# A hybrid mixer layer: another order of the output product's parts, raw weights of the last product in the space of earlier ones, and factor work kept behind the weights

## The chip, the cores and the metric

One core of a Trainium2 chip. The metric is the device time of one execution in microseconds; of several executions the median is given. The engines are TensorE (PE, matmuls), VectorE (DVE), ScalarE (ACT), GpSimd (POOL) and SyncE (SP), each with a queue of instructions that it works off in order. SP issues nearly all loads, POOL the stores that are spoken of below.

## The reference

One decoder layer on 1024 tokens of width 1024, all in float32:

```python
mod = c_act @ w_ada[l] + b_ada[l]
h = rms_norm(x) * (1.0 + scale1) + shift1
proj = h @ w_in[l]
y_ssd = ssd_branch(...)
y_mlstm = mlstm_branch(...)
merged = g_ssd * (y_ssd @ w_branch_ssd[l]) + g_mlstm * (y_mlstm @ w_branch_mlstm[l])
x = x + gate1 * (merged @ w_out[l])
h2 = rms_norm(x) * (1.0 + scale2) + shift2
gt, up = jnp.split(h2 @ w_ffn_in[l], 2, axis=-1)
x = x + gate2 * ((jax.nn.silu(gt) * up) @ w_ffn_out[l])
return rms_norm(x) * final_norm_w
```

The two branches are a Mamba-2 scan and an xLSTM matrix memory. The five large products behind them (`w_branch_ssd`, `w_branch_mlstm`, `w_out`, `w_ffn_in`, `w_ffn_out`) are what the change is about.

## The kernel before

**Number format.** Each float32 operand of a product is split into a high part (a cast on ACT to a rounded 32-bit form, `fp32r`) and the rest (a subtraction on DVE), and each product is three matmuls: high by high, high by rest, rest by high. For the input projection `split` does this for a raw tile of weights (`raw` into `wh` and `wl`, lines 124 and 125).

**Strassen's scheme.** The large products are done in seven part products of half the size each way instead of eight. The sums of weight blocks (S1 to S4) and plain blocks (A11, A12, A22) are the factors. They are prepared ahead, while the mixers run from about 623 to 1385 us: `prep_steps` loads two rows of blocks (`pr`, lines 197 and 198), makes four sums on DVE (lines 210 to 213), and `put_pair` casts, subtracts and stores each factor (lines 162 to 164) through one of two `pf` buffers into DRAM (`fac_ssd`, `fac_ml`, `fac_out`, `fac_ffn`; `f1_d` for part of `w_ffn_in`). Of `w_ffn_out` the blocks A11, A12, A22 aren't stored as factors, and `strassen` loads them raw (`wt`, line 850) and splits them on the way.

**The products.** `strassen` (line 831) goes through the parts in the given `order`. For each of them it takes weights `wf` and tokens `tf` (cast on ACT at line 825, subtraction on DVE at line 826), runs 12 matmuls for each block row `k` (line 879) into four PSUM banks, and hands each bank to a `sink` that adds it to sums. The output product runs from 1909 to 1988 us, and `out_sink` makes the new residual `x1` from it: tokens 0 to 511 are complete after part 4, tokens 512 to 1023 after part 5. Behind it `feat` transposes a block of 128 features of 512 tokens on PE (line 272) and ACT copies it out with scale and shift (line 273) into one of five `f` buffers. The eight features of the first half are split into `h0` and also stored to `f0_d` (line 1124), and those of the second half enter a loop of four rounds (lines 1132 to 1148) that loads the first half again (`b11`, `b21`, lines 1134 and 1135) and builds the token factors `tf` for FFN-in. `head` computes, for the first rows of FFN-in, the two parts that need only the first half.

**FFN-in** (2065 to 2440 us) loads raw columns (`rw`) of each next block, makes their sums on POOL (lines 1109 to 1112), splits them into `sw`, and runs five parts for each block (line 1074); the gated result goes to `act_d` in DRAM (lines 1182 and 1189). The FFN-out product loads it again (`bt`, line 1213) and ends in the final norm.

**What sets the order.** The program is written as one sequence, and a scheduler with a timeline model puts the instructions of each engine in order, within the dependencies; the pools decide in which space a tile lies, and a tile whose space was another's waits until that is free. `tc.issue_after(x)` keeps what is written inside it behind `x` in that order.

Of the kernel before, what the change touches and what calls it, by code (L numbers as in the profile page):

```python
# [9 lines left out]
F32 = mybir.dt.float32  # L10
# [5 lines left out]
P = 128  # L16
# [21 lines left out]
def hybrid_layer(ctx: ExitStack, tc: tile.TileContext, a: dict, out: bass.AP, dbg=None):  # L38
# [27 lines left out]
    def f(ap):  # L66
        return ap.bitcast(F32)
# [50 lines left out]
    V.tensor_scalar(cact, cact, 0.5, None, MUL)  # L118


    def split(raw):
        wh = wp.tile([P, 1024], F32R, name="wh", bufs=NWH)
        wl = wp.tile([P, 1024], F32R, name="wl", bufs=NWL)
        A.copy(wh, raw)  # L124
        V.tensor_tensor(wl, raw, f(wh), SUB)  # L125
        return wh, wl
# [4 lines left out]
    def wload(src):  # L131
        raw = raw_tile()
        Q.dma_start(k8(raw), src.rearrange("(k p) n -> p k n", p=P))
        wh, wl = split(raw)
        return k8(wh), k8(wl)
# [24 lines left out]
    def put_pair(dst, r):  # L160
        m = pf()
        A.copy(m[:, 0], r)  # L162
        V.tensor_tensor(m[:, 1], r, f(m[:, 0]), SUB)  # L163
        G.dma_start(dst, f(m))
# [23 lines left out]
    def prep_steps(name, gate=None):  # L188
        fd, w_d = fac_d[name], w_of[name]
        n = fd.shape[0]  # L190

        def put(r, kk, fa):
            put_pair(fd[kk, FA[fa]], r)

        for kk in range(n):
            r0, r1 = ld("pr"), ld("pr")
            Q.dma_start(r0, w_d[kk * P:(kk + 1) * P, :])
            Q.dma_start(r1, w_d[(kk + n) * P:(kk + n + 1) * P, :])
            if gate is not None:
                g = f(pf()).rearrange("p two n -> p (two n)")  # L200
                Q.dma_start(g, gr_d[gate:gate + 1, :].broadcast_to([P, D]))
                for r in (r0, r1):
                    V.tensor_tensor(r, r, g, MUL)
                yield
            a11, a21, a12, a22 = r0[:, 0:512], r0[:, 512:], r1[:, 0:512], r1[:, 512:]
            if fd.shape[1] == 7:
                for fa, x in (("A11", a11), ("A12", a12), ("A22", a22)):
                    put(x, kk, fa)
                    yield
            V.tensor_tensor(a22, a21, a22, ADD)  # L210
            V.tensor_tensor(a21, a11, a21, SUB)
            V.tensor_tensor(a11, a22, a11, SUB)  # L212
            V.tensor_tensor(a12, a12, a11, SUB)
            yield
            for fa, x in (("S2", a11), ("S3", a21), ("S4", a12), ("S1", a22)):
                put(x, kk, fa)
                yield
# [612 lines left out]

    def strassen(name, load, order, sink, wq, nw, tq, nt, wt_, t2_, rows=False, odd=0):

# [166 lines left out]
    x1 = {}  # L999
    U, U3, R = {}, {}, {}  # L1000

# [21 lines left out]
    def out_sink(p, i, bank):  # L1023
        if p == 1:
            U[i] = ut()
            A.copy(U[i], bank)
            V.tensor_tensor(x1_half(0, i, 0), U[i], x_rows(0, i, 0), ADD)
        elif p == 3:
            R[i] = po.tile([P, 512], F32, name="r", tag="r", bufs=4)
            V.tensor_tensor(R[i], bank, x_rows(1, i, 0), ADD)  # L1030
        elif p == 2:
            x1_part(0, i, 0, bank, x1_half(0, i, 0))
        elif p == 6:
            V.tensor_tensor(U[i], bank, U[i], ADD)
        elif p == 7:
            U3[i] = ut()
            V.tensor_tensor(U3[i], bank, U[i], ADD)
            V.tensor_tensor(x1_half(0, i, 1), U3[i], x_rows(0, i, 1), ADD)
            V.tensor_tensor(R[i], R[i], U[i], ADD)
            V.tensor_tensor(U3[i], U3[i], x_rows(1, i, 1), ADD)  # L1040
        elif p == 4:
            x1_part(0, i, 1, bank, x1_half(0, i, 1))
            x1_done(0, i)
        else:
            x1_part(1, i, 0, bank, R[i])
            x1_part(1, i, 1, bank, U3[i])
            x1_done(1, i)

    strassen("out", lambda k, i, j: am[k + 4 * i], (1, 3, 2, 6, 7, 4, 5), out_sink, wq, 6, tq, 5, None,
             lambda: po.tile([P, 512], F32, name="t2", tag="t2", bufs=2), rows=True)  # L1050
    ctxO.close()
    ctxU.close()


# [63 lines left out]

    f0_d = tc.dram_tile([KD, P, 512], F32, name="f0_d")
    h0 = []  # L1120
    for k in range(KD):
        t = feat(0, k)
        h0.append(split_pair(t, hlo, "h0", "h0", KD))
        G.dma_start(f0_d[k], t)
    w5 = []
    for fa in ("S2", "S3", "S1", "A22", "S4"):
        m = ps_.tile([P, 2, 512], F32R, name="sw", tag="sw", bufs=5)
        Q.dma_start(f(m), f1_d[0, FA[fa]])
        w5.append((m[:, 0], m[:, 1]))
    heads = [head(j) for j in range(NHEAD)]  # L1130
    tf = {n: [] for n in ("t2", "t3", "t1", "t4", "b22")}
    for k in range(4):
# [64 lines left out]
    wq, tq = pool(ctx, "wring"), pool(ctx, "tring")  # L1197
    pb = [pool(ctx, "b0"), pool(ctx, "b1")]
    po = pool(ctx, "fin", "right")
    g2 = po.tile([P, D], F32, name="g2")  # L1200
    Q.dma_start(g2, gr_d[1:2, :].broadcast_to([P, D]))
    fw = po.tile([P, D], F32, name="fw")
    Q.dma_start(fw, a["final_norm_w"].unsqueeze(0).broadcast_to([P, D]))
    ssf = [po.tile([P, 4, 8], F32, name=f"ssf{i}") for i in range(2)]
    yts = [po.tile([P, 1024], F32, name="yt", tag="yt", bufs=8) for _ in range(8)]
    V2, V3 = {}, {}
    acts = {}

# [13 lines left out]
    def y_part(tj, i, ci, bank, u, x=None):  # L1222

        y = yts[4 * tj + i][:, halves(ci)]
        if x is None:
            V.tensor_tensor(y, bank, g2[:, halves(ci)], MUL)
            x = u
        else:
            V.tensor_tensor(y, bank, u, ADD)
            V.tensor_tensor(y, y, g2[:, halves(ci)], MUL)  # L1230
        V.tensor_tensor(y, y, x, ADD)
        half_square(po, yts[4 * tj + i], ssf[tj][:, i], ci)

    def y_done(tj, i):
        yt, ss, t = yts[4 * tj + i], ssf[tj][:, i], 4 * tj + i
        row_rms(ss)
        for ci in range(2):
            ns = halves(ci)
            V.scalar_tensor_tensor(yt[:, ns], yt[:, ns], ss[:, 3:4], fw[:, ns], MUL, MUL)
            Q.dma_start(out[0, t * P:(t + 1) * P, ns], yt[:, ns])  # L1240

    def ffn_sink(p, i, bank):
# [10 lines left out]
        elif p == 5:  # L1253
            V.tensor_tensor(V2[i], bank, V2[i], ADD)
            y_part(1, i, 1, bank, V3[i], x1_rows(1, i, 1))
            V.tensor_tensor(V2[i], V2[i], g2[:, L_], MUL)
            V.tensor_tensor(V2[i], V2[i], x1_rows(1, i, 0), ADD)
# [3 lines left out]
        else:  # L1261
            y_part(1, i, 0, bank, V2[i])
            y_done(1, i)

    strassen("ffn", act_load, ORDER, ffn_sink, wq, 5, tq, 6, lambda: po.tile([P, 512], F32, name="wt", tag="wt", bufs=4),
             lambda: po.tile([P, 512], F32, name="t2", tag="t2", bufs=1), rows=True)
# [23 lines left out]
```

## Time and profile before

| | |
|---|---|
| time, median of 3 runs | 2674.37 us (2671.96 to 2679.69) |
| the profiled execution, its time | 2680.4 us |
| its span | 2678.7 us |
| mean granted clock of TensorE | 0.978 |
| PE busy | 2535.8 us (95%) |
| DVE busy | 1771.2 us (66%) |
| ACT busy | 1102.3 us (41%) |
| POOL busy | 439.9 us (16%) |
| DRAM traffic over the span | 180 GB/s |

A busy share is a mean over the whole span. PE isn't busy for 2678.7 - 2535.8 = 142.9 us of it, spread over stretches with different limits; the rows below are taken from three of them.

### The profile page before, as it was taken

What the parts mean: (1) busy time and instruction counts of PE and PEld (TensorE: products, weight loads), DVE (VectorE), ACT (ScalarE), POOL (GpSimd) and SP (SyncE); (2) the same over time, 40 slices, a digit from 0 to 9 for tenths busy, and PEclk for the clock granted to TensorE, in tenths of its full rate; (3) what the DMA queues carried; (4) which work ended last, traced back from release to release, by engine and by line L of the source; (5) the groups of instructions that cost most, each with busy time, mean ns of one, the idle gap of its engine ahead of it and who ended that gap; (6) DMA issues with size and microseconds to landing.
All of it is one profiled execution on the core that took longest, in us unless ns stands there. A gap on an engine that the chain in (4) does not pass through costs nothing.

```text
span 2678.7 us, 35176 instructions
## 1 busy us (share of the span) xinstructions
PE 2535.8 (95%) x12907; PEld 2117.0 (79%) x12907; DVE 1771.2 (66%) x2885; ACT 1102.3 (41%) x2016; POOL 439.9 (16%) x508
## 2 busy tenths in 40 slices
PE   5999999999999998999999989999998999997998
PEld 3788777888878797888789877878876888886886
DVE  8577767786787567657653537575767666666847
ACT  5455544453444344444443444443244322322323
POOL 4000112110142111212211310000011333231000
PEclk9999999999999999999999999999999999998999
DMA  6323332355778877766753366754773433326655
GB/s 201 102 83 115 114 106 84 110 170 183 233 257 286 287 233 252 257 231 206 248 196 93 116 243 223 268 190 158 249 263 120 126 97 116 101 88 241 218 167 195
DMA packets 342965, 484.04 MB, mean 181 GB/s; under 512 B 21985, under 2 KB 224065, under 8 KB 342793
## 3 DMA queue, kind: packets, MB, share of 16 engines
q1 hardware_dynamic: 309752, 364.87, 43.3%
q0 software_dynamic: 33040, 116.93, 11.6%
q8 instruction: 101, 1.65, 0.3%
q14 instruction: 72, 0.58, 0.1%
HBM read 343.01 MB, written 138.72 MB: 180 GB/s over the span
## 4 chain that ended last, share of the span: by engine, by line
PE 56%; issue 16%; DMA 11%; DVE 9%; ACT 4%; POOL 3%; SPq 0%; POOLq 0%; DVEq 0%; ACTq 0%
PE mm L364 14%; PE n L879 10%; PE n L1074 8%; PE mm L879 5%; PE sc L879 5%; PE mm L1074 4%; PE sc L1074 4%; PE mm L642 2%; DMA ab<-acs_d 1%; DMA raw<-in_w_in_dram 1%; DMA pr<-in_w_ffn_out_dram 1%; ACT ab L546 1%; DVE red L231 1%; DMA fac_out<-pf 1%; PE n L573 1%
## 5 line engine op out<-in xcount | busy, mean ns | idle before, releaser
L364 PE MATMUL mm<-hh,wh 128*128 128x512 f32 x1392 | 557.8, 401 | 15.1 <-ACT xf L378 9.6
L364 PE MATMUL mm<-hh,wl 128*128 128x512 f32 x1392 | 554.3, 398 | 0.0
L364 PE MATMUL mm<-hl,wh 128*128 128x512 f32 x1392 | 553.4, 398 | 0.0
L364 PEld LDWEIGHTS mm<-hh,wh 128*128 128x128 f32 x1392 | 266.1, 191 | 72.8 <-ACT xf L378 11.8
L364 PEld LDWEIGHTS mm<-hh,wl 128*128 128x128 f32 x1392 | 265.8, 191 | 53.2 <-DVE wl L125 0.7
L364 PEld LDWEIGHTS mm<-hl,wh 128*128 128x128 f32 x1392 | 265.9, 191 | 51.8 <-issue 0.2
L125 DVE TENSOR_TENSOR wl<-raw,wh 128x1024 fp32r<-128x1024 f32 x122 | 151.6, 1243 | 89.5 <-PE mm L642 26.1
L124 ACT CAST wh<-raw 128x1024 fp32r<-128x1024 f32 x122 | 127.4, 1045 | 158.3 <-DMA raw<-in_w_in_dram 61.1
L162 ACT CAST pf<-pr 128x512 fp32r<-128x512 f32 x149 | 89.6, 619 | 211.5 <-DVE pr L212 75.6
L826 DVE TENSOR_TENSOR tf<-bt,tf 128x512 fp32r<-128x512 f32 x162 | 110.0, 686 | 94.8 <-ACT tf L825 94.7
L386 DVE SCALAR_TENSOR_TENSOR xf<-cr,pk,xf 128x1023 f32<-128x1023 f32 (+2 forms) x120 | 159.9, 1334 | 17.0 <-ACT xf L378 15.7
L163 DVE TENSOR_TENSOR pf<-pr,pf 128x512 fp32r<-128x512 f32 x149 | 101.2, 694 | 99.7 <-ACT pf L162 99.5
L879 PE MATMUL n<-tf,wf 128*128 128x512 f32 x672 | 158.0, 393 | 4.7 <-ACT tf L825 4.1
L825 ACT CAST tf<-bt 128x512 fp32r<-128x512 f32 x162 | 99.9, 619 | 138.0 <-PE sc L879 74.1
L879 PEld LDWEIGHTS n<-tf,wf 128*128 128x128 f32 x672 | 127.3, 190 | 32.3 <-ACT tf L825 4.5
L1074 PE MATMUL n<-t,sw 128*128 128x512 f32 x552 | 137.9, 395 | 4.2 <-ACT t L825 4.2
L1074 PEld LDWEIGHTS n<-t,sw 128*128 128x128 f32 x552 | 104.1, 189 | 27.7 <-ACT t L825 5.7
L879 PE MATMUL n<-wf,tf 128*128 128x512 f32 x540 | 124.8, 389 | 0.0
L879 PEld LDWEIGHTS n<-wf,tf 128*128 128x128 f32 x540 | 101.3, 188 | 21.3 <-DVE wf L826 0.3
L546 ACT ACTIVATE ab<-ab,gsum 128x128 f32<-128x128 f32 x256 | 78.4, 389 | 83.5 <-DMA ab<-acs_d 75.0
L879 PE MATMUL mm<-wf,tf 128*128 128x512 f32 x360 | 93.1, 394 | 14.6 <-ACT tf L825 14.6
L825 ACT CAST sw<-rw 128x512 fp32r<-128x512 f32 x84 | 51.4, 620 | 113.9 <-POOL rw L1111 51.0
(411 smaller groups left out, 4960.3 us busy)
## 6 DMA issues: line engine op xcount, KB each, us to landing
raw<-in_w_in_dram SPq DMA_DIRECT2D x104, 512.0 KB, 4.3
fac_ffn<-pf POOLq DMA_DIRECT2D x44, 512.0 KB, 5.4
wf<-fac_ffn SPq DMA_DIRECT2D x44, 512.0 KB, 4.2
rw<-in_w_ffn_in_dram SPq DMA_DIRECT2D x42, 512.0 KB, 4.1
raw<-in_w_ada_dram SPq DMA_DIRECT2D x40, 512.0 KB, 6.1
tg_d<-tz POOLq DMA_DIRECT2D x64, 256.0 KB, 5.4
ab<-acs_d SPq DMA_DIRECT2D x32, 512.0 KB, 4.1
fac_ssd<-pf POOLq DMA_DIRECT2D x32, 512.0 KB, 5.7
```

Source lines behind the costliest of these rows:

```text
L124: A.copy(wh, raw)
L125: V.tensor_tensor(wl, raw, f(wh), SUB)
L162: A.copy(m[:, 0], r)
L163: V.tensor_tensor(m[:, 1], r, f(m[:, 0]), SUB)
L364: T.matmul(ps, lhsT=ww[:, k, :], rhs=xx[:, halves(hf)], start=n == 0, stop=n == 23)
L386: V.scalar_tensor_tensor(dst[:, sh:], cr[:, :S - sh], cw[:, 3 - sh, ti:ti + 1], dst[:, sh:], MUL, ADD)
L546: A.activation(ab[q][:, e, c], ab[q][:, e, c], AF.Relu, scale=-1.0, bias=acs_t[:, 4 * q + c, h0 + e:h0 + e + 1])
L642: T.matmul(ps[:, c], lhsT=hT[k][x_][:, sl], rhs=ws[k // 4][w_][:, k % 4], start=n == 0, stop=n == 23)
L825: A.copy(m[:, 0], t)
L826: V.tensor_tensor(m[:, 1], t, f(m[:, 0]), SUB)
L879: T.matmul(bk[i], lhsT=st[:, x, sl], rhs=mv[:, y], start=k == 0 and m == 0, stop=k == n - 1 and m == 2)
L1074: T.matmul(bank, lhsT=ww[:, k, :], rhs=b[k][:, r_], start=k == 0 and n == 0, stop=k == 3 and n == 2)
```

## The change

It has three parts.

- **Factor work behind the weights.** `mark` keeps the last written load (`mark[0]`), cast (`mark[1]`) and subtraction (`mark[2]`) of a tile of weights of the input projection. The loads `pr`, the casts and subtractions in `put_pair` and the four sums in `prep_steps` are written inside `behind(i)`, so the scheduler keeps each behind that mark on its engine. `prep_ffn1`'s sums and the stores are as before.
- **The output product** takes its parts in the order (1, 2, 6, 7, 4, 3, 5) and not (1, 3, 2, 6, 7, 4, 5). The extra sums `R` (four buffers) go, since `U` can hold them by then. `first_half`, which makes the first half's features, `h0` and the stores to `f0_d`, is called by `strassen` before its seventh part, and the first heads are written behind the four rounds of the `tf` build instead of ahead of them.
- **FFN-out's start.** The raw tiles `wt` get a pool of their own, `wo`, opened first on the right side, in the space that the raw weights of the input projection and of FFN-in had. The two rows `g2` and `fw` are loaded where they are first used.

```diff
+    mark = [None, None, None]
+
+    def behind(i):
+        return tc.issue_after(getattr(mark[i], "ins", mark[i]))
...
-        A.copy(wh, raw)
-        V.tensor_tensor(wl, raw, f(wh), SUB)
+        mark[1] = A.copy(wh, raw)
+        mark[2] = V.tensor_tensor(wl, raw, f(wh), SUB)
...
-        Q.dma_start(k8(raw), src.rearrange("(k p) n -> p k n", p=P))
+        mark[0] = Q.dma_start(k8(raw), src.rearrange("(k p) n -> p k n", p=P))
...
-        A.copy(m[:, 0], r)
-        V.tensor_tensor(m[:, 1], r, f(m[:, 0]), SUB)
+        with behind(1):
+            A.copy(m[:, 0], r)
+        with behind(2):
+            V.tensor_tensor(m[:, 1], r, f(m[:, 0]), SUB)
...
-            Q.dma_start(r0, w_d[kk * P:(kk + 1) * P, :])
-            Q.dma_start(r1, w_d[(kk + n) * P:(kk + n + 1) * P, :])
+            with behind(0):
+                Q.dma_start(r0, w_d[kk * P:(kk + 1) * P, :])
+                Q.dma_start(r1, w_d[(kk + n) * P:(kk + n + 1) * P, :])
...
-            V.tensor_tensor(a22, a21, a22, ADD)
-            V.tensor_tensor(a21, a11, a21, SUB)
-            V.tensor_tensor(a11, a22, a11, SUB)
-            V.tensor_tensor(a12, a12, a11, SUB)
+            with behind(2):
+                V.tensor_tensor(a22, a21, a22, ADD)
+                V.tensor_tensor(a21, a11, a21, SUB)
+                V.tensor_tensor(a11, a22, a11, SUB)
+                V.tensor_tensor(a12, a12, a11, SUB)
...
         for q, p in enumerate(order):
+            if ahead is not None and q == 6:
+                ahead()
...
         elif p == 3:
-            R[i] = po.tile([P, 512], F32, name="r", tag="r", bufs=4)
-            V.tensor_tensor(R[i], bank, x_rows(1, i, 0), ADD)
+            V.tensor_tensor(U[i], bank, U[i], ADD)
...
-            V.tensor_tensor(R[i], R[i], U[i], ADD)
             V.tensor_tensor(U3[i], U3[i], x_rows(1, i, 1), ADD)
+            V.tensor_tensor(U[i], U[i], x_rows(1, i, 0), ADD)
...
-            x1_part(1, i, 0, bank, R[i])
+            x1_part(1, i, 0, bank, U[i])
...
+    def first_half():
+        for k in range(KD):
+            t = feat(0, k)
+            h0.append(split_pair(t, hlo, "h0", "h0", KD))
+            G.dma_start(f0_d[k], t)
+
+    strassen("out", lambda k, i, j: am[k + 4 * i], (1, 2, 6, 7, 4, 3, 5), out_sink, wq, 6, tq, 5, None,
+             lambda: po.tile([P, 512], F32, name="t2", tag="t2", bufs=2), rows=True, ahead=first_half)
...
-    heads = [head(j) for j in range(NHEAD)]
...
         put("b22", b22)
+    heads = [head(j) for j in range(NHEAD)]
...
+    wo = pool(ctx, "wraw", "right")
     po = pool(ctx, "fin", "right")
-    g2 = po.tile([P, D], F32, name="g2")
-    Q.dma_start(g2, gr_d[1:2, :].broadcast_to([P, D]))
-    fw = po.tile([P, D], F32, name="fw")
-    Q.dma_start(fw, a["final_norm_w"].unsqueeze(0).broadcast_to([P, D]))
...
-    strassen("ffn", act_load, ORDER, ffn_sink, wq, 5, tq, 6, lambda: po.tile([P, 512], F32, name="wt", tag="wt", bufs=4),
+    strassen("ffn", act_load, ORDER, ffn_sink, wq, 5, tq, 6, lambda: wo.tile([P, 512], F32, name="wt", tag="wt", bufs=4),
```

**SP at the start of FFN-out.** The loads in the order of SP's queue, before; `rw` are the last columns of FFN-in, `xr` rows of `x1`, `g` the row `g2`.

```order
L154 DMA rw<-in_w_ffn_in_dram 128x8x128 x12
L1201 DMA g_20396<-gr_d 128x1024
L1203 DMA fw<-in_final_norm_w_dram 128x1024
L850 DMA wt<-in_w_ffn_out_dram 128x512 x4
L988 DMA xr<-x_d 128x512 x4
L850 DMA wt<-in_w_ffn_out_dram 128x512 x4
L1213 DMA bt<-act_d 128x512 x8
L850 DMA wt<-in_w_ffn_out_dram 128x512
L1213 DMA bt<-act_d 128x512 x18
```

And with the change:

```order
L159 DMA rw<-in_w_ffn_in_dram 128x8x128 x5
L859 DMA wt<-in_w_ffn_out_dram 128x512 x4
L159 DMA rw<-in_w_ffn_in_dram 128x8x128 x3
L859 DMA wt<-in_w_ffn_out_dram 128x512 x5
L159 DMA rw<-in_w_ffn_in_dram 128x8x128 x4
L999 DMA xr<-x_d 128x512
L1222 DMA g_20910<-gr_d 128x1024
L999 DMA xr<-x_d 128x512 x3
L1222 DMA fw<-in_final_norm_w_dram 128x1024
L1232 DMA bt<-act_d 128x512 x18
L859 DMA wt<-in_w_ffn_out_dram 128x512
L1232 DMA bt<-act_d 128x512 x5
```

Nine of the loads `wt` moved ahead of the last `rw`, the two rows moved between and behind the `xr`, and no `wt` stands between them and the first 18 loads `bt`.

**PE at the end of the output product.** `wf,tf` are the matmuls of its last part, `ident,x1t` the transposes of the features, `h,wl` the first matmuls of the heads. Before:

```order
L879 MATMUL mm<-wf,tf 128x512 x12
L879 MATMUL sc<-wf,tf 128x512 x12
L272 MATMUL n_17050<-ident,x1t 128x128
L272 MATMUL n_17071<-ident,x1t 128x128
L272 MATMUL n_17050<-ident,x1t 128x128 x2
L272 MATMUL n_17071<-ident,x1t 128x128 x2
L272 MATMUL n_17050<-ident,x1t 128x128
L272 MATMUL n_17071<-ident,x1t 128x128
L272 MATMUL n_17050<-ident,x1t 128x128 x4
L272 MATMUL n_17092<-ident,x1t 128x128 x4
L272 MATMUL n_17071<-ident,x1t 128x128 x4
L272 MATMUL n_17113<-ident,x1t 128x128 x4
```

And with the change:

```order
L890 MATMUL mm<-wf,tf 128x512 x5
L281 MATMUL n_16916<-ident,x1t 128x128 x4
L890 MATMUL mm<-wf,tf 128x512 x7
L890 MATMUL sc<-wf,tf 128x512 x3
L281 MATMUL n_16937<-ident,x1t 128x128 x4
L890 MATMUL sc<-wf,tf 128x512 x9
L281 MATMUL n_16916<-ident,x1t 128x128 x4
L281 MATMUL n_16958<-ident,x1t 128x128 x4
L281 MATMUL n_16937<-ident,x1t 128x128 x4
L281 MATMUL n_16979<-ident,x1t 128x128 x4
L281 MATMUL n_16958<-ident,x1t 128x128 x4
```

Two features' transposes moved into the last part; the next ones stand behind its last nine matmuls.

**DVE in the mixers, around one tile of weights.** `pr` and `pf` are factor work, `wl` the rest of the weights, `xf` and `sm` are the mixers' own. Before:

```order
L386 SCALAR_TENSOR_TENSOR xf<-cr,pk_109,xf 128x1021
L728 RECIPROCAL sm_8878<-sm_8878 128x1
L210 TENSOR_TENSOR pr<-pr 128x512
L211 TENSOR_TENSOR pr<-pr 128x512
L212 TENSOR_TENSOR pr<-pr 128x512
L388 SCALAR_TENSOR_TENSOR xf<-cr,xf 128x1024
L213 TENSOR_TENSOR pr<-pr 128x512
L266 TENSOR_SCALAR sm_8878<-sm_8878 128x1
L163 TENSOR_TENSOR pf<-pr,pf 128x512 x2
L732 TENSOR_TENSOR sm_8878<-sm_8878 128x1
L125 TENSOR_TENSOR wl<-raw,wh 128x1024
L386 SCALAR_TENSOR_TENSOR xf<-cr,pk_109,xf 128x1023
```

And the same place with the change, found by the operations on `sm_8878`:

```order
L694 SCALAR_TENSOR_TENSOR qw<-xf,md 128x128 x2
L741 TENSOR_TENSOR sm_8878<-sm_8878 128x1
L395 SCALAR_TENSOR_TENSOR xf<-cr,pk_109,xf 128x1021
L397 SCALAR_TENSOR_TENSOR xf<-cr,xf 128x1024
L750 SCALAR_TENSOR_TENSOR yb<-og,sc 128x4x128
L130 TENSOR_TENSOR wl<-raw,wh 128x1024
L170 TENSOR_TENSOR pf<-pr,pf 128x512 x2
L395 SCALAR_TENSOR_TENSOR xf<-cr,pk_109,xf 128x1023
L395 SCALAR_TENSOR_TENSOR xf<-cr,pk_109,xf 128x1022
L395 SCALAR_TENSOR_TENSOR xf<-cr,pk_109,xf 128x1021
L397 SCALAR_TENSOR_TENSOR xf<-cr,xf 128x1024
L170 TENSOR_TENSOR pf<-pr,pf 128x512 x5
```

The four sums on `pr` are not there any more, and the two `pf` stand behind `wl`; further on five `pf` stand in a row.

## Rows read from the trace of the kernel before

**Rows 1.** The table of stretches (from:to, us, busy and (instructions), clock, DMA share, GB/s).
```profile
869.00:1385.00 516.00, 488.43 (x2723) 420.03 (x2722) 328.14 (x598) 218.58 (x384) 98.85 (x166) 0.98 0.74 245
1385.00:1490.00 105.00, 104.40 (x704) 96.04 (x703) 47.06 (x90) 40.46 (x72) 20.56 (x19) 1.00 0.33 99
...
1988.00:2065.00 77.00, 62.26 (x269) 48.55 (x268) 56.95 (x87) 45.01 (x80) 13.68 (x18) 0.91 0.55 184
2065.00:2437.00 372.00, 372.00 (x1631) 305.79 (x1631) 241.20 (x331) 105.52 (x168) 129.79 (x120) 1.00 0.33 101
```

**Rows 2.** What PE waited for, 1988 to 2065 (total us, times, longest).
```profile
PE n L1074 <- ACT f L273: 3.8, 1, 3.8
```

**Rows 3.** The timeline around FFN-in's features (start, us, engine, line, [idle before]).
```profile
1989.84 0.62 ACT L825 CAST h<-f 128x512 fp32r<-128x512 f32 x1
...
1990.21 0.58 POOL L1124 DMA_DIRECT2D f_d<-f  x1 [5.29 <-ACT f L273]
...
1998.03 1.45 ACT L273 ACTIVATE f<-n,mod 128x512 f32<-128x512 f32 x2 [2.63 <-DMA f_d<-f]
...
2001.40 0.78 ACT L273 ACTIVATE f<-n,mod 128x512 f32<-128x512 f32 x1 [0.90 <-PE n L272]
...
2014.65 0.69 DVE L1140 TENSOR_TENSOR b<-f,b 128x512 f32<-128x512 f32 x1
...
2036.04 0.69 DVE L1140 TENSOR_TENSOR b<-f,b 128x512 f32<-128x512 f32 x1 [1.49 <-DMA b<-f_d]
...
2041.52 4.25 SPq L154 DMA_DIRECT2D rw<-in_w_ffn_in_dram  x3
...
2043.24 0.69 DVE L1140 TENSOR_TENSOR b<-f,b 128x512 f32<-128x512 f32 x1 [1.57 <-DMA b<-f_d]
...
2057.91 1.22 PE L1074 MATMUL mm<-t,sw 128*128 128x512 f32 x2 [3.61 <-ACT sw L825]
```

**Rows 4.** The table of stretches, behind PE's wait at 2057.91.
```profile
2057.80:2061.20 3.40, 3.29 (x8) 2.62 (x9) 3.40 (x4) 2.20 (x5) 1.85 (x2) 0.50 0.52 173
```

**Rows 5.** The table of stretches, end of FFN-in and start of FFN-out.
```profile
2440.50:2443.50 3.00, 0.00 (x0) 0.00 (x0) 2.08 (x3) 0.63 (x1) 0.53 (x1) 1.00 0.93 294
2443.50:2455.00 11.50, 0.00 (x0) 0.00 (x0) 3.40 (x5) 3.71 (x6) 0.54 (x1) 0.50 1.03 386
2455.00:2460.60 5.60, 5.55 (x13) 4.40 (x14) 4.07 (x6) 3.11 (x6) 0.00 (x0) 0.50 1.05 387
```

**Rows 6.** The timeline, end of FFN-in and start of FFN-out.
```profile
2437.61 2.88 PE L1074 MATMUL sc<-b,sw 128*128 128x512 f32 x12
...
2440.95 2.55 SPq L988 DMA_DIRECT2D xr<-x_d  x4
...
2449.24 4.82 SPq L1213 DMA_DIRECT2D bt<-act_d  x8
...
2454.38 1.96 ACT L825 CAST tf<-bt 128x512 fp32r<-128x512 f32 x3 [2.09 <-DMA bt<-act_d]
...
2455.05 1.22 PE L879 MATMUL mm<-wf,tf 128*128 128x512 f32 x2 [14.56 <-ACT tf L825]
```

**Rows 7.** What PE waited for, 869 to 1385.
```profile
PE n L714 <- ACT kw L703: 5.9, 3, 4.9
PE mm L642 <- DVE wl L125: 4.2, 1, 4.2
...
PE mm L364 <- ACT tz L394: 3.8, 3, 2.4
```

**Rows 8.** What ACT waited for, 869 to 1385.
```profile
ACT pf L162 <- DMA fac_out<-pf: 20.1, 11, 4.2
ACT pf L162 <- DMA fac_ffn<-pf: 19.9, 9, 5.6
```

**Rows 9.** The timeline, 1163 to 1172.
```profile
1165.67 1.14 ACT L162 CAST pf<-pr 128x512 fp32r<-128x512 f32 x2 [1.91 <-DVE pr L212]
...
1169.90 2.39 PE L642 MATMUL mm<-wl,hh 128*128 128x256 f32 x11 [4.25 <-DVE wl L125]
```

More of the change, by code (lines that the diff above doesn't have):

```diff
@@ L829, in hybrid_layer, with strassen @@
     L_, H_ = halves(0), halves(1)
-    def strassen(name, load, order, sink, wq, nw, tq, nt, wt_, t2_, rows=False, odd=0):
+    def strassen(name, load, order, sink, wq, nw, tq, nt, wt_, t2_, rows=False, odd=0, ahead=None):
         fd, w_d = fac_d[name], w_of[name]
@@ L999, in hybrid_layer @@
     x1 = {}
-    U, U3, R = {}, {}, {}
+    U, U3 = {}, {}
     def x_rows(tj, i, ci):
@@ L1044, in out_sink @@
         else:
-            x1_part(1, i, 0, bank, R[i])
+            x1_part(1, i, 0, bank, U[i])
             x1_part(1, i, 1, bank, U3[i])
             x1_done(1, i)
[L1049 to L1052, printed above, removed]
     def fx(name, tag, bufs):
@@ L1061, in feat @@
         return t
+    f0_d = tc.dram_tile([KD, P, 512], F32, name="f0_d")
+    h0 = []
+    def first_half():
[5 more added lines that the diff above has]
+             lambda: po.tile([P, 512], F32, name="t2", tag="t2", bufs=2), rows=True, ahead=first_half)
+    ctxO.close()
+    ctxU.close()
     ctxF = ExitStack()
@@ L1117, in wpair @@
         return m[:, 0], m[:, 1]
[L1119 to L1124, printed above, removed]
     w5 = []
@@ L1206, in hybrid_layer, with row, gate2 @@
     V2, V3 = {}, {}
-    acts = {}
+    acts, rows = {}, {}
+    def row(name, src):
+        if name not in rows:
+            rows[name] = po.tile([P, D], F32, name=name)
+            Q.dma_start(rows[name], src.broadcast_to([P, D]))
+        return rows[name]
+    def gate2():
+        return row("g2", gr_d[1:2, :])
     def act_load(k, i, j):
@@ L1225, in y_part @@
         if x is None:
-            V.tensor_tensor(y, bank, g2[:, halves(ci)], MUL)
+            V.tensor_tensor(y, bank, gate2()[:, halves(ci)], MUL)
             x = u
@@ L1229, in y_part @@
             V.tensor_tensor(y, bank, u, ADD)
-            V.tensor_tensor(y, y, g2[:, halves(ci)], MUL)
+            V.tensor_tensor(y, y, gate2()[:, halves(ci)], MUL)
         V.tensor_tensor(y, y, x, ADD)
@@ L1238, in y_done @@
             ns = halves(ci)
+            fw = row("fw", a["final_norm_w"].unsqueeze(0))
             V.scalar_tensor_tensor(yt[:, ns], yt[:, ns], ss[:, 3:4], fw[:, ns], MUL, MUL)
@@ L1255, in ffn_sink @@
             y_part(1, i, 1, bank, V3[i], x1_rows(1, i, 1))
-            V.tensor_tensor(V2[i], V2[i], g2[:, L_], MUL)
+            V.tensor_tensor(V2[i], V2[i], gate2()[:, L_], MUL)
             V.tensor_tensor(V2[i], V2[i], x1_rows(1, i, 0), ADD)
```

## The prediction

> **What bounds the kernel now.** I read the table of stretches first [rows 1]. TensorE (PE) sets the time: from 2065 to 2437 us it is busy for all of 372 us, at a granted clock of 1.00. So an edit can only earn where PE waits, or where the clock is at 0.50 because PE waited just before. Four stretches matter. From 869 to 1385 us (the mixers, with the preparation of factors beside them) PE is idle for 516.00 - 488.43 = 27.6 us, and the clock's mean of 0.98 costs about 0.02 x 516 = 10 us more. From 1385 to 1490 it is idle for 0.6 us. From 1988 to 2065 (output product to FFN-in) it is idle for 14.7 us, and 0.09 x 77 = 6.9 us go to the clock. At the start of the FFN-out product PE is idle for 14.56 us [rows 6]. A wait in another engine counts here only if PE's waits name it.
>
> **Start of FFN-out.** PE's last matmuls of FFN-in run 2.88 us from 2437.61, so to 2440.49; the next matmul is at 2455.05, after an idle 14.56 us that ACT's cast `tf` ended, and that cast had waited for the load of `bt` [rows 6]. The reader is to see why `bt` is late: SP issues it only at 2449.24, behind the raw weights `wt`, whose second four could go only when the first four had been cast. The row that bounds it is thus the place of `bt` in SP's queue and not the transfer itself, 2449.24 to 2454.38 = 5.14 us.
>
> After the change nine `wt` loads stand among the last loads of FFN-in's weights, and the casts of five of them ahead of the last activations on ACT. They fall before 2437, where the 16 DMA engines are busy 0.33, ACT 105.5 of 372 us and DVE 241.2 of 372 us [rows 1]; five casts and five subtractions are about 5 x 0.62 = 3.1 us on ACT (the cast's length in [rows 3]) and as much on DVE, in room for tens of us. Without that cover they would cost the 3 us again. SP now holds ahead of the first `bt`: four `xr` (2.55 us for four [rows 6]) and the two row loads (under 0.5 us each by the spacing of SP's rows, say 0.4). The third of these six waits for the third of the last twelve matmuls, 2437.61 + 3 x 0.24 = 2438.3. From there three `xr`, 1.9, and one row, 0.4: first `bt` at 2440.6. With the same 5.14 us it lands at 2445.8; a cast of 0.62 and PE starts at about 2446.5 to 2447.5. Gain: 2455.05 - 2447 = **8 us**. Bounds: the loads just ahead are 2 MB, so if `bt` takes 8 us, 5 us are left; if it goes out without any wait, 10. The restart at half clock stays, since PE still idles 6.5 us and the clock fell 3.0 us after PE stopped [rows 5]: the stretch from 2455.00 to 2460.60 at 0.50 moves forward as it is. The rows `g2` and `fw` are loaded later than before but used only when a whole product is done, behind more than 25 us of matmuls: 0.
>
> The Trainium skill ("DMA: Bandwidth & Descriptors", Issuing engines are not separate DMA queues) says that transfers of all issuing engines run on the same 16 DMA engines and interleave. The trace agrees: 2443.5 to 2455 has a DMA share of 1.03 at 386 GB/s [rows 5]. By that rate 2 MB ahead of `bt` are an estimated 5.2 us, which would put PE at 2447 too.
>
> **End of the output product.** The order (1,2,6,7,4,3,5) does the same seven products of about 11 us, and the same count of DVE operations, since the sum in `R` becomes one in `U`. Nothing waits in PE's rows of products with this beginning elsewhere, so 0 (bound: one DVE operation, 0.7 us, per bank of four, up to 3). What it buys is time: tokens 0 to 511 are done two products before the end instead of one.
>
> Now the features. Before, all eight of the first half come after the last product: ACT needs 0.78 for the copy out of PSUM and 0.62 for the cast, so 1.4 us each, and from the sixth on the five `f` buffers are full: the store issued at 1990.21 ends ACT's wait of 2.63 at 1998.03 (7.8 us), and PE waits 3.8 us for it [rows 2, 3]. After the change two features stand inside the last product, among its last 19 matmuls (the first four or five us before its end); the other six still stand behind its last matmuls, because the order shows the next transposes only there. Two stores therefore leave 3 to 5 us earlier, the third at about 1990.9 as before, and the eighth feature, which needs the third buffer, comes at about 1999 to 2000 and not at 2001.4: 1.5 to 2.5 us.
>
> The larger piece is the heads, which now stand behind the build of `tf`. Before, the four rounds of the build begin on DVE at 2014.65 and the fourth at 2043.24: 28.6 us, 9.5 per round, with ACT and DVE work of heads between and the reload of `b` as the last wait [rows 3]. Without heads between, I take the spacing at which the last two rounds stand, about 7.2 us each, plus 2 for a reload that is not ready: 24 us. The first round comes earlier by the 2 us above and 2 to 3 more, since ACT has no head copies and no cast of raw weights ahead of it: about 2010. Fourth round: 2010 + 24 = 2034, 9 us earlier. `rw` was issued at 2041.52, right behind the last reload, so it too comes 7 us or more earlier, and POOL's sums have no store of `act_d` between them; the wait of 3.61 us before 2057.91 [rows 3], at which PE waits for `sw`, vanishes, and so does half of the 3.4 us at clock 0.50 behind it [rows 4].
>
> The heads' matmuls have to be somewhere: of the 77 us from 1988 to 2065, 77 - 14.7 - 6.9 = 55.4 are work at full clock, so PE alone could be 21.6 us earlier, and doesn't bind first. By my walk through the new order, with the durations of the same rows of before, heads, their activations and the last rounds end at 2047 to 2049, and the matmul of 2057.91 comes at 2050 to 2052. Six to eight, plus 1.7 for the clock: **8 us**. Bounds: -1, if the reloads and stores land so late that only the first feature's time is won, and -12 from the fourth round's 9 with 3.6.
>
> **Factor work behind the weights.** Casts, subtractions and loads of the factors no longer may be put ahead of the last weight's load, cast and subtraction that the program has written before them. No operation is added. The order shows nothing changed up to about 869 us; from there the factors fall back by 20 to 110 us, and their last ones move past 1385, into 1385 to 1490, where ACT is busy 40.5 and DVE 47.1 of 105 us [rows 1]: that is their cover. Some 30 casts of 0.62 and as many subtractions of 0.69 fit there; if they don't, PE meets them one at a time at 0.6 to 1.3 us.
>
> PE's waits here: 5.9 us for `kw` on ACT, and 4.2 for one `wl` on DVE [rows 7]. The `wl` case is the one that the rule excludes: ACT's two factor casts at 1165.67 stand ahead of `wh`, six factor operations on DVE ahead of `wl`, and PE goes on at 1169.90 after 4.25 [rows 9]. In the new order `wl` is ahead of the factor rows there: -4.3, and a half-clock restart of 1.7. The `kw` case is not excluded: a factor cast waits for a store to free one of two `pf` buffers, and what stands behind it on ACT waits too. There were 20 such waits on two factor tensors alone, 40 us, the longest 5.6 [rows 8]; few reached PE, at 2.4 for `tz` to 4.9 for `kw` [rows 7]. In the new order other operations stand behind other casts, so I expect about the same count, in other places. Factors spaced a little wider should make it rarer; a new stretch makes room for more. I take **-2**, bounds -10 (all of them gone, with their clock) and +9 (two or three more).
>
> **Sum.** 8 + 8 + 2 = 18 us from the profiled execution of 2680.4 us (span 2678.7): 2662. That execution is 6 us above the median of 2674.4, and the kernel's three runs spread over 8 us; the same 18 from the median gives **2657 us**. A measurement of this kernel can tell about 0.3%, 8 us, from no change: faster is below 2666, slower above 2682.
>
> **Rivals.**
> 1. Both boundaries gain, the mixers stay within 8 us: 0.55, 2649 to 2667, centre 2657.
> 2. The output end gives nothing, because the stores of features still land in 7 to 8 us beside the loads of `sw`, and the first round waits for the same things. For it: six of the eight features haven't moved, and five `f` buffers are as many as before. Against it: the head's work between the rounds is gone by order. Only 8 + 2 are left: 2664 to 2668. 0.15. The page of the skill that I named speaks for it: if stores and loads share the engines, an earlier store finds them as full. Here 1988 to 2065 moved on without a full share, so I believe it for single stores only.
> 3. The other side: factor casts that wait for `pf` buffers stop ACT ahead of operations that PE needs. Each such case costs 2.4 to 4.9 us of idle [rows 7], and about 2 more where a restart at half clock follows as after 2057.91 [rows 4], some 5 together. Three or four more than before take the 16 back to nothing; from five on the kernel is slower, at 2683 or more. For it: the falling back makes factor work pile up (five subtractions in a row stand in the new DVE order), and the longest waits are already 5.6. Against: it has room from 1385 on. 0.18: 0.10 for no change (2667 to 2682), 0.08 beyond.
> 4. The mixers' waits mostly go, -10 or more with the boundaries, or PE nears its floor at the output end: 2638 to 2648. 0.12.
>
> Faster by over 0.3%: nearly all of 1, 4 and half of 2, 0.73. Within: 0.19. Slower: 0.08. Range: from 2641, in case 4, to 2674, in the middle of case 3's return to nothing; what is beyond either end holds about 2 in 10.
>
> **What would show it.** FFN-out: first `bt` issued about 2 to 4 us after FFN-in's last group began, PE idle 6 to 8 us in place of 14.56. Output end: PE's idle in the 77 us after the last product at 5 to 9 and not 14.7, `sw` no longer the releaser, the four rounds within 24 us. Mixers: no wait on `wl` with factor rows ahead, and 1385 to 1490 still full. The prediction is wrong if PE's idle from 869 to 1490 rises by over 10 us, if the first `bt` waits for a landing that I have not seen in the queue, or if the rounds keep a spacing of 9.5 us without heads between.

## The result and the profile after

The changed kernel takes 2646.99 us (median of 6 runs, 2641.29 to 2654.09) against 2675.24 us (6 runs): ratio 0.9898, 95% interval 0.9882 to 0.9914, so 27 us less (23 to 32). The forecast was 2657 us, 18 us less by its sum. The profiled execution is the longest of the six, 2654.09 us with a span of 2652.4; its places are compared with those of before, and the sizes are checked with the runs below.

The total was forecast about right, and its terms were not. The page of the changed kernel, its span and PE's line of part 1:

```profile
span 2652.4 us, 35144 instructions
...
PE 2531.1 (95%) x12907; PEld 2111.2 (80%) x12907; DVE 1781.9 (67%) x2885; ACT 1102.0 (42%) x2016; POOL 448.4 (17%) x508
```

PE has the same 12907 matmuls, so the same matmul by number marks the same place in both executions, except at the output end: there the order changed, and it marks the same count of matmuls (1966.90 lies 2 us ahead of the product's end). The table of stretches of the changed kernel, cut at the matmuls at which [rows 1] were cut; the third row is 1490 to 1625 of before, the sixth the start of FFN-out:

```profile
869.10:1355.00 485.90, 476.93 (x2722) 413.75 (x2721) 309.06 (x565) 210.16 (x369) 90.10 (x148) 1.00 0.69 230
1355.00:1466.60 111.60, 107.64 (x704) 96.97 (x703) 73.05 (x124) 47.91 (x88) 30.83 (x37) 1.00 0.68 224
1466.60:1601.80 135.20, 125.67 (x616) 104.66 (x615) 71.36 (x151) 68.08 (x121) 22.75 (x27) 0.95 0.55 193
...
1966.90:2041.40 74.50, 65.39 (x269) 49.19 (x269) 52.53 (x84) 43.32 (x77) 12.76 (x16) 0.89 0.55 185
2041.40:2418.00 376.60, 373.89 (x1631) 306.96 (x1630) 251.88 (x339) 109.68 (x174) 134.01 (x121) 1.00 0.36 110
2418.00:2444.10 26.10, 18.13 (x71) 14.48 (x70) 15.13 (x24) 8.92 (x15) 1.08 (x2) 0.80 0.91 317
```

Read against [rows 1], length by length. The mixers take 485.90 and not 516.00 us, **30 less**: PE's idle falls from 27.6 to 9.0 us and the clock is 1.00. The next stretch takes 111.60 and not 105.00, **6.6 more**. The output end takes 74.50 and not 77.00, 2.5 less, but FFN-in behind it 376.60 and not 372.00, 4.6 more: together **2 more**. FFN-out's start takes 26.1 us; with the same matmuls in 33.0 before, **7 less**. Together 28 us less, of which 2 are lost again elsewhere: the two profiled executions lie 26.3 us apart.

**FFN-out's start went as forecast.** The timeline:

```profile
2418.91 2.43 PE L1093 MATMUL sc<-b,sw 128*128 128x512 f32 x10
...
2421.17 11.06 SPq L1232 DMA_DIRECT2D bt<-act_d  x12
...
2428.63 0.62 ACT L834 CAST tf<-bt 128x512 fp32r<-128x512 f32 x1 [5.59 <-DMA bt<-act_d]
...
2429.30 1.22 PE L890 MATMUL mm<-wf,tf 128*128 128x512 f32 x2 [7.97 <-ACT tf L834]
```

The first `bt` goes out 0.2 us before PE's last matmul ends (2421.34); forecast was 0.1 us behind it, and before it was 8.75 us. It needs 7.46 us and not 5.14 to land, so PE idles 7.97 us where I had 6.5, in place of 14.56 [rows 6]. While it is under way, the table of stretches has, before and then with the change:

```profile
2449.20:2454.40 5.20, 0.00 (x0) 0.00 (x0) 0.69 (x1) 0.64 (x2) 0.00 (x0) 0.50 1.05 394
```

```profile
2421.20:2428.70 7.50, 0.14 (x1) 0.00 (x0) 2.51 (x4) 0.70 (x2) 1.08 (x2) 0.67 0.93 289
```

About the same bytes are moved (2.05 and 2.17 MB), at 289 and not 394 GB/s.

**The mixers' waits are gone.** What PE waited for from 869 to 1355, the three largest, and what ACT waited for there before a factor's cast, for a store that frees its buffer:

```profile
PE sc L745 <- ACT ht L742: 2.5, 2, 1.4
PE mm L373 <- DVE wl L130: 1.8, 2, 1.0
PE n L723 <- DVE kw L713: 1.5, 2, 1.1
```

```profile
ACT pf L168 <- DMA fac_out<-pf: 23.4, 11, 5.1
...
ACT pf L168 <- DMA fac_ffn<-pf: 6.6, 4, 4.7
```

The `kw` wait of 4.9 us, the `wl` wait of 4.2 and the `tz` wait of 2.4 [rows 7] have no successor above 1.4. Yet ACT still waits 15 times, 30 us, for the two stores, where it was 20 times and 40 us [rows 8]: these waits went on, and PE hardly met one.

Fewer operations of the factors are left in the stretch. Those that touch their rows `pr` (us, busy time and count on DVE, on ACT, clock, DMA share, GB/s), before in the mixers, then with the change in the mixers and in the next stretch:

```profile
869.00:1385.00 516.00, 135.91 (x195) 63.34 (x105) 0.98 0.74 245
```

```profile
869.10:1355.00 485.90, 110.77 (x156) 51.61 (x85) 1.00 0.69 230
1355.00:1466.60 111.60, 28.58 (x41) 11.91 (x20) 1.00 0.68 224
```

On DVE 156 of 195 stay and on ACT 85 of 105. The rest stands in the next stretch, where before had one on DVE and none on ACT.

**The output end moved its waits.** DVE's rounds and what stands between them, the store and the wait behind:

```profile
1993.03 0.69 DVE L1152 TENSOR_TENSOR b<-f,b 128x512 f32<-128x512 f32 x1 [1.38 <-ACT f L282]
...
2000.22 0.69 DVE L1152 TENSOR_TENSOR b<-f,b 128x512 f32<-128x512 f32 x1 [1.48 <-DMA b<-f_d]
...
2009.25 0.69 DVE L1152 TENSOR_TENSOR b<-f,b 128x512 f32<-128x512 f32 x1 [0.72 <-DMA b<-f_d]
...
2012.99 1.22 DVE L130 TENSOR_TENSOR wl<-raw,wh 128x1024 fp32r<-128x1024 f32 x1
...
2018.27 0.68 DVE L1117 TENSOR_TENSOR v<-n,u 128x512 f32<-128x512 f32 x1
2019.32 0.69 DVE L1152 TENSOR_TENSOR b<-f,b 128x512 f32<-128x512 f32 x1 [0.36 <-DMA b<-f_d]
...
2042.08 0.54 POOL L1202 DMA_DIRECT2D act_d<-u  x1 [4.78 <-DVE u L1201]
...
2048.00 0.69 DVE L1117 TENSOR_TENSOR v<-n,u 128x512 f32<-128x512 f32 x1 [6.22 <-DMA act_d<-u]
...
2055.28 1.19 PE L1093 MATMUL n<-t,sw 128*128 128x512 f32 x2 [2.71 <-DVE u L1184]
```

The last matmuls of the output product, before and then with the change, and with the change ACT's copy of the eighth feature of the first half:

```profile
1985.33 2.89 PE L879 MATMUL sc<-wf,tf 128*128 128x512 f32 x12
```

```profile
1966.63 2.33 PE L890 MATMUL sc<-wf,tf 128*128 128x512 f32 x9
...
1980.46 0.78 ACT L282 ACTIVATE f<-n,mod 128x512 f32<-128x512 f32 x1 [0.55 <-PE n L281]
```

The product ends at 1968.96, and the eighth feature comes 11.5 us behind it; before it was 2001.40 - 1988.22 = 13.2 [rows 3]. The rounds are spaced 7.2, 9.0 and 10.1 us, 26.3 for the three: the heads' rows (`v` and the raw weights' `wl`) still stand between them. The wait of 3.61 us for `sw` [rows 3] is gone, as forecast. In its place the fifth head's `v` waits 6.22 us on DVE for the store of `act_d` that frees a head's buffer, and PE waits 2.71 us for what is queued behind it. It goes on at half clock:

```profile
2055.20:2057.00 1.80, 1.72 (x4) 1.46 (x5) 1.77 (x4) 0.00 (x0) 0.00 (x0) 0.50 0.57 165
```

So in place of the wait and the half-clock stretch that were to vanish [rows 3, 4], others stand 14 us into FFN-in, and are its 4.6 us more.

### The profile page after: what moved, and what is told of

It reads as the page before. It is cut to its first block, busy times and chain, and to the rows that moved or that the text cites. A ratio compares the mean times of both kernels' runs of the same rounds, so it can differ in the third digit from the quotient of the medians.

```text
span 2652.4 us, 35144 instructions
## 1 busy us (share of the span) xinstructions
PE 2531.1 (95%) x12907; PEld 2111.2 (80%) x12907; DVE 1781.9 (67%) x2885; ACT 1102.0 (42%) x2016; POOL 448.4 (17%) x508
## 3 DMA queue, kind: packets, MB, share of 16 engines
q0 software_dynamic: 33040, 116.93, 11.5%
## 4 chain that ended last, share of the span: by engine, by line
PE 55%; issue 16%; DMA 11%; DVE 11%; ACT 4%; POOL 3%; SPq 0%; POOLq 0%; DVEq 0%; ACTq 0%
PE mm L373 16%; PE n L890 10%; PE n L1093 8%; PE mm L890 5%; PE sc L890 5%; PE mm L1093 4%; PE sc L1093 3%; DMA raw<-in_w_in_dram 1%; DMA fac_ffn<-pf 1%; DMA ab<-acs_d 1%; DVE wl L130 1%; DVE pf L170 1%; DMA fac_ml<-pf 1%; PE n L705 1%; PE n L582 1%
## 5 line engine op out<-in xcount | busy, mean ns | idle before, releaser
L130 DVE TENSOR_TENSOR wl<-raw,wh 128x1024 fp32r<-128x1024 f32 x122 | 153.2, 1256 | 83.5 <-PE mm L373 34.3
```

The costliest lines, as they stand in the source:

```text
L130: mark[2] = V.tensor_tensor(wl, raw, f(wh), SUB)
```

## The experiments

All ratios are to the kernel before, on the same chip and in the same rounds; microseconds are worked out from the ratio and before's median of the same runs (2671 to 2676). The groups of runs below were on different chips, so kernels of different groups are compared by their ratios.

**The parts alone.** Each part of the diff put into the kernel before. Of FFN-out's start (cut; the two rows are loaded at first use as in the change):

```diff
+    wo = pool(ctx, "wraw", "right")
...
-    strassen("ffn", act_load, ORDER, ffn_sink, wq, 5, tq, 6, lambda: po.tile(
+    strassen("ffn", act_load, ORDER, ffn_sink, wq, 5, tq, 6, lambda: wo.tile(
```

> Only the start of FFN-out is changed (pool for the raw tiles, rows loaded at first use). Both the reading of the two traces and the prediction give 6 to 9 us less: PE's idle at the start of FFN-out goes from 14.6 to about 8 us. A rival, that the loads of bt meet other transfers without the earlier parts, would leave under 3 us.

Measured: 0.9986 (0.9975 to 0.9997), 4 us less (1 to 7). PE's one wait there:

```profile
PE mm L879 <- ACT tf L825: 7.7, 1, 7.7
```

The wait is halved as expected, from 14.6; the stretch takes 26.3 us in place of 33.0. That the time fell by 4 and not by 7 is within the interval of the ratio, which doesn't exclude the rival's 3 us; the wait speaks against it. On top of the factor work's part (below, 0.9894 against 0.9921) this part is worth 7, but those two intervals overlap.

The output product's part alone (cut; the first half's features ahead of the last part and the sums in `U` as in the change):

```diff
-    strassen("out", lambda k, i, j: am[k + 4 * i], (1, 3, 2, 6, 7, 4, 5), out_sink,
+    strassen("out", lambda k, i, j: am[k + 4 * i], (1, 2, 6, 7, 4, 3, 5), out_sink,
...
-    heads = [head(j) for j in range(NHEAD)]
...
         put("b22", b22)
+    heads = [head(j) for j in range(NHEAD)]
```

> Only the output product's order, the first half ahead of its last part and the heads behind the tf build. The prediction's term says 8 us less. The trace of the changed kernel says nothing gained: -1 to +3 us, because the features are bound by ACT and the f stores as before, the rounds are still 7 to 10 us apart, and a new wait of the second FFN-in block on the store of act_d takes 2.7 us and a half-clock stretch.

Measured: 1.0022 (1.0010 to 1.0035), 6 us more (3 to 9). The table of stretches, output end and FFN-in:

```profile
1975.90:2055.70 79.80, 66.54 (x269) 50.59 (x268) 53.56 (x84) 42.55 (x76) 12.58 (x16) 0.87 0.55 175
2055.70:2428.90 373.20, 372.33 (x1631) 305.84 (x1630) 246.22 (x334) 107.42 (x170) 131.92 (x122) 1.00 0.33 102
```

79.8 + 373.2 = 453.0 us where before has 77 + 372 = 449 [rows 1]: 4 more. The clock is 0.87, and not 0.91. My forecast of 8 us less is refuted, in its sign too. The wait of 2.7 us behind DVE that I expected from the changed kernel's trace isn't here, though; PE's wait there is 0.9 us, and it waits 2.1 us for a load of the heads' weights:

```profile
PE n L1084 <- DMA wl<-f_d: 2.1, 1, 2.1
...
PE n L1084 <- DVE u L1175: 0.9, 1, 0.9
```

So the cause of the 6 us isn't shown by that one wait.

The factor work's part alone (cut; the loads and the four sums are kept behind their marks too):

```diff
+        with behind(1):
+            A.copy(m[:, 0], r)
+        with behind(2):
+            V.tensor_tensor(m[:, 1], r, f(m[:, 0]), SUB)
```

> Only the factor work kept behind the weights. The prediction's term says 2 us less (between 10 less and 9 more). The trace of the changed kernel says 20 to 24 us less: nearly all of PE's idle from 869 to 1385 us gone (27.6 to under 10 us, and no half-clock stretch there), some 7 us given back between 1385 and 1550.

Measured: 0.9921 (0.9905 to 0.9937), 21 us less (17 to 25). The three stretches from the mixers to the first product's start:

```profile
867.60:1351.00 483.40, 476.01 (x2722) 413.44 (x2722) 308.92 (x565) 209.89 (x368) 89.79 (x148) 1.00 0.70 232
1351.00:1462.30 111.30, 107.74 (x703) 96.97 (x702) 73.00 (x124) 47.62 (x88) 30.83 (x37) 1.00 0.68 224
1462.30:1598.10 135.80, 125.67 (x616) 104.49 (x615) 71.00 (x151) 68.18 (x121) 22.73 (x27) 0.95 0.56 192
```

33 us less in the mixers, 6 back behind them. Most of the change's gain is this part.

**FFN-out's start and the factor work together**, with the output end as before.

> The first and the third part without the changes at the output product. If the parts add up and the output product's part gives nothing or costs, this is as fast as the whole change or up to 3 us faster: 27 to 31 us less than before. If the output product's part earns 8 us as predicted, it is 8 us slower than the whole change: about 20 us less than before.

Measured: 0.9894 (0.9874 to 0.9914), 28 us less (23 to 34), beside 0.9898 for the whole change: the output product's part is not needed for the gain.

**What of the rule helps.** Each of its three kinds of mark alone, and the rule with another pace of the steps that it orders. Only the loads:

```diff
+            with behind(0):
+                Q.dma_start(r0, w_d[kk * P:(kk + 1) * P, :])
+                Q.dma_start(r1, w_d[(kk + n) * P:(kk + n + 1) * P, :])
```

> Only the loads of the factors' rows are kept behind the weights' loads; casts, sums and subtractions are free. In the order the casts ahead of four points of the mixers are 60, 90, 121 and 147 of 149, where before has 66, 99, 125 and 149 and the full rule 58, 87, 110 and 135. Theory place (what helps is that no factor operation stands ahead of a weight's cast and subtraction): no more than 5 us less, since nothing on ACT and DVE is ordered. Theory spacing (what helps is that the same factor work is spread over a longer time, so that ACT and DVE are free more often): a part of the full rule's 21, some 5 to 12 us less.

Only the casts (`with behind(1)` around `A.copy` in `put_pair`):

> Only the factors' casts on ACT are kept behind the weights' casts; loads and DVE are free. Spacing in the order: 60, 87, 113, 137, nearly that of the full rule. Theory place: about half, 5 to 12 us less, since DVE's factor rows may stand ahead of the weights' subtraction as before. Theory spacing: nearly all of it, 15 to 22 us less.

The whole rule with the steps written earlier:

```diff
-        for _ in range(2):
+        for _ in range(3):
             next(preps, None)
```

> The full rule, but the factor steps are written earlier in the program (three steps behind each product of the mixers in place of two), so that the weights that they stand behind are earlier ones. Spacing in the order: 62, 93, 123, 149, nearly that of before; the rule holds for each step. Theory place: the full gain, 17 to 23 us less. Theory spacing: little, 0 to 8 us less, with PE's waits of 869 to 1385 mostly there.

The whole rule with the steps written later:

```diff
-                for _ in range(3):
+                for _ in range(2):
                     next(preps, None)
```

> The full rule, and the factor steps are written later (two steps and not three for each quarter of the values), so that they are spread further: 52, 74, 97, 116, 133 where the full rule has 58, 87, 110, 135, 149. Theory place: as the full rule, 21 us less. Theory spacing: at least as much gain up to 1300 us, PE idle there under 9 us, and factor work of the last 16 casts meets the stretch up to 1550, where some of it is given back: 17 to 26 us less in all.

Only DVE's sums and subtractions (`with behind(2)`):

> Only the factors' sums and subtractions on DVE are kept behind the weights' subtraction; loads and casts are free. Spacing in the order: 58, 87, 111, 135, that of the full rule. With casts alone PE still waited for scm on DVE (1.7, 2.95 and 1.89 us) and no longer for kw or wl. If spacing alone decides, this is as the full rule: 18 to 22 us less. If each engine's part takes away that engine's waits, scm and wl are gone here, waits for tz, kw or wh on ACT of 2 us or more stay, and the time is about 10 us less, so that the two engines' parts add up to the full rule.

| kernel | ratio (95%) | us | mixers, us | DVE operations in them | next stretch, us |
|---|---|---|---|---|---|
| steps earlier, whole rule | 1.0002 (0.9986 to 1.0018) | 0 | 508.5 | 596 | 108.6 |
| loads only | 0.9978 (0.9966 to 0.9989) | -6 | 498.0 | 581 | 108.4 |
| casts only | 0.9960 (0.9947 to 0.9973) | -11 | 493.0 | 565 | 111.9 |
| DVE only | 0.9946 (0.9927 to 0.9966) | -14 | 487.6 | 565 | 113.6 |
| whole rule | 0.9921 (0.9905 to 0.9937) | -21 | 483.4 | 565 | 111.3 |
| steps later, whole rule | 0.9962 (0.9947 to 0.9977) | -10 | 479.8 | 536 | 117.8 |

The last three columns are from rows like these, of the table of stretches: "steps earlier" and "steps later" (two rows each, and for the latter a third).

```profile
866.30:1374.80 508.50, 482.94 (x2722) 418.20 (x2722) 325.20 (x596) 217.07 (x382) 96.97 (x163) 0.98 0.73 243
1374.80:1483.40 108.60, 105.82 (x704) 97.61 (x703) 51.30 (x95) 42.06 (x76) 22.89 (x24) 0.98 0.39 122
```

```profile
858.40:1338.20 479.80, 475.33 (x2722) 416.16 (x2721) 292.61 (x536) 203.06 (x352) 80.66 (x133) 1.00 0.63 211
1338.20:1456.00 117.80, 109.23 (x704) 98.05 (x703) 75.57 (x125) 47.61 (x85) 31.21 (x37) 0.99 0.66 216
1456.00:1609.20 153.20, 132.41 (x616) 109.94 (x615) 97.01 (x190) 78.35 (x143) 34.77 (x47) 0.89 0.77 264
```

In the mixers of before stand 598 DVE operations in 516.0 us [rows 1], and with the part for FFN-out alone, where that order is the same, 598 in 511.2, with the output product's part alone 599 in 509.8. So a single profile scatters by 6 us there, and 508.5 is no gain.

- To stand behind the weights written before it isn't enough: with the steps written earlier this holds for every factor operation, and 596 of 598 DVE operations stay in the stretch; the time is that of before. The theory of place forecast 17 to 23 us less. Built without the rule, this kernel has the same order on PE, DVE, ACT and SP, so the marks move nothing in it.
- The fewer factor operations fall into the mixers, the shorter they are, down to 479.8 us with 536. What leaves goes into the next stretches, which get longer; with the steps later the third is 153.2 against 135 us, and the net is 10 less (6 to 14) and not 21. In that third stretch stand 37 operations on `pr` on DVE and 20 on ACT, where before had none, and a long wait for `kw`, like that of before in the mixers [rows 7], is there too:

```profile
PE n L723 <- ACT kw L712: 5.0, 1, 5.0
```

- The count isn't all either: casts only, DVE only and the whole rule have the same 565, and 493.0, 487.6 and 483.4 us. Casts only is apart from the whole rule, by its ratio too; DVE only lies between, and its ratio is apart from neither. PE's longest waits suggest why. With only the casts ordered, waits for DVE stay; with only DVE ordered, waits for ACT stay, and one for a `tz` of DVE's own:

```profile
PE n L702 <- DVE scm L678: 4.8, 2, 3.0
PE mm L370 <- ACT xf L384: 1.9, 2, 1.2
```

```profile
PE sc L743 <- ACT ht L740: 3.7, 3, 2.6
PE mm L371 <- DVE tz L608: 2.9, 1, 2.9
```

Waits for `scm` aren't among those of DVE only in this stretch, and waits for `ht` not among those of casts only. My forecast for DVE only, "about 10 us less, so that the two engines' parts add up", was low by 4; 11 and 14 add up to 25, and the whole is 21, which the intervals don't tell apart. Each alone already brings the count to 565.

Neither theory forecast all of it. Loads only (6) and steps earlier (0) came out as spacing said, casts only (11) as place said, and steps later (10) below both.

One rival is left. The factors' loads and stores leave the stretch with their operations: 245 GB/s in the mixers before [rows 1], 232 with the whole rule, 211 with the steps later. The runs don't separate fewer operations on ACT and DVE from less DMA traffic. Against traffic as the main cause speaks that PE's waits in the mixers name ACT and DVE and no load, before and after, and that casts only moves as many bytes there as the whole rule (228 GB/s in 493.0 us, 232 in 483.4) and takes longer.

**The output product's part taken apart**, on top of the two others. Only the heads written later:

> Parts one and three, and of the output product's part only the heads written behind the tf build. Beside it the first and third part alone gave 0.9894 of before. Theory heads (what the output end loses is that the heads come late, so that the second block of FFN-in meets DVE waiting for the store of act_d): 2 to 4 us more than the first and third part alone, and a wait of PE for DVE of 2 us or more in the second block. Theory features (what it loses is the features and the order): no more than 1 us away from the first and third part alone.

Only the order and the first half ahead of the last part:

> Parts one and three, and of the output product's part the order (1, 2, 6, 7, 4, 3, 5) and the first half ahead of the last part, with the heads written as before. Theory heads: the features come some 2 us earlier and nothing is lost behind them, 0 to 2 us less than the first and third part alone. Theory features: 2 to 4 us more, with a longer half-clock stretch around the features' transposes.

The whole on the same chip:

> The whole change once more, on the same chip as the two partial ones. If the output product's part costs 3 us, as the first runs let expect (0.9898 against 0.9894 for the first and third part, and 1.0022 for it alone), this is within 2 us of the slower of the two partial kernels; if it earns the 8 us predicted, it is 8 us faster than the first and third part.

Measured: heads 0.9893 (0.9877 to 0.9909), order and first half 0.9905 (0.9887 to 0.9922), whole 0.9902 (0.9885 to 0.9920): 2643.05, 2646.43 and 2646.07 us. None is apart from the others or from the two other parts without it (0.9894). PE's waits at the output end, heads later and then order and first half, the rows that tell them apart:

```profile
PE n L1083 <- DVE u L1180: 1.8, 1, 1.8
...
PE n L1083 <- DMA wl<-f_d: 1.2, 1, 1.2
```

```profile
PE mm L1093 <- ACT sw L834: 5.3, 1, 5.3
PE n L1093 <- ACT t L834: 3.8, 4, 1.5
```

With the heads later the wait for `sw` is gone and a wait behind DVE's held queue stands there, 1.8 us; without it the wait for `sw` grows from 3.6 to 5.3. That is the trade that theory "heads" named, but its 2 to 4 us more are not there: heads later is as fast as without, and the order and the first half are 3 us slower, as theory "features" had it. Which of the two costs the 6 us of the part put in alone stays open all the same: the intervals are wider than the differences here.

## Why the prediction was right, and where not

**The total** came out from one right term, one of wrong sign and one far too small: -8, -8, -2 were forecast, and the parts alone measured -4 (in its stretch -7), +6 and -21. That the total lay near the forecast is luck: the output end was forecast 14 us too good and the mixers 19 us too poor, and these errors mostly cancel. The parts alone add up to 19 us less and the whole is 27, with intervals of 3 to 5 us on each; the 6 us that the output product's part costs alone don't show on top of the two others, and why stays open.

**FFN-out's start, 8 us: right in mechanism, and 7 in size.** `bt` goes out when forecast. The term mis-sized is its landing, 7.46 us and not 5.14. The Trainium skill ("DMA: Bandwidth & Descriptors", Issuing engines are not separate DMA queues) has all transfers run interleaved on the same 16 engines; the trace agrees that they are nearly full there (share 0.93 while `bt` is under way). My estimate of 5.2 us went by 386 GB/s, and it was 289: the rate failed and not the bytes. What lowered it stays open; the row `fw` goes out right ahead of `bt`, and two stores of `act_d` just behind it, and no run takes them apart.

**The output end, 8 us: wrong.** The features did as forecast, 1.7 us earlier against the product's end. The step that failed is "Without heads between, I take the spacing at which the last two rounds stand, about 7.2 us each". The heads are written behind the loop, but the scheduler still places them between its rounds, as the new DVE order shows; the first round came 2 us earlier against the product's end and not 5, the next three took 26.3 us and not 24, and the fourth came 50.4 us after the product where it was 55.0: 5 earlier and not 9. Second, I looked at the wait that goes (3.61 us) and not at what is late next: the fifth head needs the first head's buffers, and those wait for the store of `act_d`. The Trainium skill (Trainium Kernel Development and Optimization, Best Practices) says that consistent bubbles can mean that on-chip memory ran out. What this trace has is no consistent bubble but a single one: 6.22 us on DVE, for one of the eight head buffers. So it neither bears the sentence out nor speaks against it. Rival 2 named this term's outcome at 0.15.

**The mixers, 2 us: the mechanism half right, the size wrong.** The failed step is "so I expect about the same count, in other places". I counted ACT's waits for the `pf` buffers as the cause of PE's, and since the rule doesn't shorten them I left the gain at the one `wl` case. ACT's waits did stay, 15 for 85 casts where it was 20 for 105. What changed is that 39 fewer operations of the factors fall into the stretch on DVE and 20 fewer on ACT. That PE's waits go because these queues have less ahead of what PE needs is the reading that fits the runs; less DMA traffic in the stretch isn't excluded. Rival 4 named the outcome at 0.12. The cover that I gave the moved work at no cost, 1385 to 1490, was not free: it takes 6.6 us more, so "1385 to 1490 still full" fell too.

**Rival 3** (casts that hold ACT, slower) didn't come; no wait on ACT above 1.4 us is left in the mixers.

What stays open: whether spreading alone, without the rule, would earn the same. Without it the pace at which the steps are written hardly moves them: written earlier or later, the built orders have at every eighth cast of a weight at most 6 of the 149 factor casts more or fewer ahead of it than before. So no run spreads them without the rule.

## What to carry to other kernels

Work that fills the gaps of a stage cost here by how much of it stood in that stage, not only by the queue that it blocked: count its operations per stretch before and after, and ask where those that leave will go, since too many of them lengthened the next stages. A place in the source isn't a place on the engine where a scheduler decides; look up in the engine's new order whether the rows that you think gone are gone. And when a wait vanishes, follow the freed engine to the next buffer that it needs.

## What the runs showed that I had not expected

The same instruction order from 869 to 1385 us took 516.0, 511.2 and 509.8 us in three executions, so a single profile of one stage can't tell 6 us. And less idle time didn't bring a higher clock at the output end: from 1966.90 to 2041.40 PE idles 74.50 - 65.39 = 9.1 us at a mean granted clock of 0.89, where before it was 14.7 us at 0.91 [rows 1]. The shorter idle is in smaller pieces: its largest is 1.3 us there, and was 3.8 [rows 2].
